# Start of a two-layer decoder kernel on one core: products of zeros ahead of the first tokens, one Newton chain for four blocks, and the first projection by contraction chunks in a written order

## The chip, the cores and the metric

The kernel runs on one core of a Trainium2 chip. The core has a matrix engine (PE, with a clock that the chip grants at one of two levels, 1.2 and 2.4 GHz), a vector engine (DVE), a scalar engine (ACT), GpSimd (POOL), and SyncE (SP), which issues nearly all DMA transfers. Each engine works through its own instruction list in order; engines wait for one another on semaphores. The metric is the device time of one execution in microseconds. For the kernel before, three executions gave a median of 1206.81 us (1206.57 to 1207.68).

## The reference

One sequence of 1024 tokens with 1024 features goes through two layers in float32. What the change touches is the head of the first layer:

```
h = rms_norm(x, g_in)                      # per token: x * rsqrt(mean(x^2) + eps) * g
z = h @ w_in                               # 256 cq | 128 ckv | 32 kpe | SWA q | SWA k | SWA v | gate
q = rms_norm(cq, g_q_a) @ w_q_up           # latent attention: low-rank queries
kv = rms_norm(ckv, g_kv_a) @ w_kv_up       #                   and keys and values
ang = positions * inv_freq                 # rotary angles, cos and sin of them turn q_pe and kpe
```

After that come dense causal latent attention with eight heads, sliding-window attention with eight heads, a gate and an output projection, then a second layer of forgetting attention with sixteen heads, its gate and output projection, and a last norm. None of the arithmetic of these is changed.

## The kernel before, in words

**Arithmetic.** Every float32 product is made of three products in a reduced float32 format: each operand is split into a high part, rounded, and a low part, the rest, and high times high, low times high and high times low are summed in one accumulator (`mm3`, L113 to L116). `split` (L99) makes the two parts from an accumulator bank: ACT casts the high part (L105), DVE subtracts it for the low part (L106). `split_sb` (L109) does it from on-chip memory: ACT casts, POOL subtracts (L111).

**Memory.** A table `TAGS` gives each kind of buffer a number of copies: raw weights `wr` have four, their high and low parts `wh` and `wl` three each. Accumulators live in eight banks, two each of `pj`, `s`, `t` and `o`.

**The start** (L510 to L800). Tokens come in blocks of 128; blocks 0 to 3 are the first half, 4 to 7 the second. `square_sum` (L141) sums squares on DVE or ACT, `inv_rms` (L118) makes the reciprocal root by an integer guess and three Newton steps, a chain of twelve small DVE instructions. `row_norm` (L560) runs it for blocks 0 and 1 together, then for block 2, then for block 3, and scales each block by its factor. `norm_T` (L200) turns the normed blocks: for each of eight contraction chunks of 128 features, four transposes on PE (products with the identity `ident`, L206) fill one bank, which is split into `hh` and `hl`. The first projection (`z_a`, the 256 columns of cq) takes blocks one after the other: per block 24 products of 256 columns into one `pj` bank (`token_project`, L181), a copy by DVE (L649), and a square sum. The second (`z_b`, 288 columns: ckv, kpe, SWA v) does the same per block into an `s` bank (copies at L698, L699, L702). The norms of cq and ckv follow (L682, L712), their transposes (L687) and splits, then the rotary tables: `rotary` (L541) computes sine and cosine on DVE and ACT, DVE copies them into four buffers `r0` (L728 to L732), PE turns each with four transposes (L735), and DVE copies the result out (L736). Next the rotated key (L746, L752), the SWA key projection (`swa_k`, weights `wh` and `wl`), and the up-projections (L771 copies their results).

**What sets the order.** In the start a scheduler decides in which order each engine takes its instructions, from its own estimate of when operands are ready; work of the two projections, transposes and small DVE chains is interleaved by it. `issue_after` holds some work back behind other work. For the main part a written list of units sets PE's order, and the scheduler sets that of the other engines.

## Time and profile before

| | |
|---|---|
| median of three executions | 1206.81 us (1206.57 to 1207.68) |
| the profiled execution | 1204.9 us, its span 1203.1 us |
| mean granted clock of PE, share of full speed | 0.993 |
| PE busy | 1161.3 us, 97% of the span, 6554 products and transposes |
| DVE, ACT, POOL busy | 738.1, 703.0 and 587.8 us (61, 58 and 49%) |
| data moved | 135.27 MB |

The span is the part of an execution that the trace covers; the rest of its time, 1.8 us, lies around it. An engine's busy share is a mean over very different stages. How to read the rows further below: a timeline row gives the start, the duration, the engine, the source line, the operation with what it writes and reads, the tile sizes, and how many such instructions follow one another; in brackets stands the idle time before it and what released it. Two rows of one engine can overlap, since instructions are pipelined: the pace is the distance between starts.

### The profile page before, as it was taken

To read this page: it belongs to the slowest core of one execution; us is meant where nothing else is said; L and a number is where in the kernel's file an instruction comes from. 1 tells how busy PE (TensorE), PEld (TensorE's weight loads), DVE (VectorE), ACT (ScalarE), POOL (GpSimd) and SP (SyncE) were. 2 spreads that over 40 slices of the span, in tenths; PEclk is the share of its full clock that TensorE was granted. 3 is DMA by queue.
4 is the path that set the end of the run, shared out by engine and by line. 5 is a ranking of instruction groups with operands and counts; after the bars stand their busy time and mean duration, and the time that the engine had idled before them with its cause. 6 is when DMAs were issued, how large, how long until landed. Compare 5 with 4: busy or idle time off the path is not lost. (4 is left out here: it accounts for less than half of the span.)

```text
span 1203.1 us, 19942 instructions
## 1 busy us (share of the span) xinstructions
PE 1161.3 (97%) x6554; PEld 1001.6 (83%) x6554; DVE 738.1 (61%) x1946; ACT 703.0 (58%) x1583; POOL 587.8 (49%) x737
## 2 busy tenths in 40 slices
PE   4999999999989999999999999999999999999997
PEld 4997888888878877889998888888888888877886
DVE  8955466676775776665004666666656666657754
ACT  5634477776764765664214667666767676766532
POOL 5501154564654554434204555656555555567452
PEclk9999999999998999999999999999999999999999
DMA  6326522453653443574313222313131223247541
GB/s 213 85 51 221 164 45 62 130 152 123 167 162 94 123 142 98 171 217 119 99 49 103 63 79 62 89 53 88 55 96 61 82 69 101 66 128 223 172 162 61
DMA packets 157084, 135.27 MB, mean 112 GB/s; under 512 B 53259, under 2 KB 121638, under 8 KB 156982
## 3 DMA queue, kind: packets, MB, share of 16 engines
q1 hardware_dynamic: 156982, 134.02, 37.0%
q8 instruction: 51, 0.84, 0.3%
q14 instruction: 51, 0.42, 0.1%
HBM read 96.43 MB, written 37.55 MB: 111 GB/s over the span
## 5 line engine op out<-in xcount | busy, mean ns | idle before, releaser
L114 PE MATMUL pj<-hh,wh 128*128 128x512 f32 (+1 forms) x792 | 321.8, 406 | 1.6 <-ACT wh L110 1.6
L116 PE MATMUL pj<-hh,wl 128*128 128x512 f32 (+1 forms) x792 | 310.9, 393 | 6.0 <-POOL wl L111 6.0
L115 PE MATMUL pj<-hl,wh 128*128 128x512 f32 (+1 forms) x792 | 310.3, 392 | 0.0
L111 POOL TENSOR_TENSOR wl<-wr,wh 128x512 fp32r<-128x512 f32 (+1 forms) x130 | 162.7, 1253 | 164.3 <-ACT wh L110 153.0
L103 DVE TENSOR_TENSOR pl<-t,ph 128x512 fp32r<-128x512 f32 (+1 forms) x320 | 179.0, 564 | 83.8 <-ACT ph L102 81.6
L276 POOL TENSOR_SCALAR r<-r,sm 128x128 f32<-128x128 f32 (+4 forms) x248 | 167.1, 681 | 127.5 <-DVE sm L323 77.5
L102 ACT CAST ph<-t 128x512 fp32r<-128x512 f32 (+1 forms) x320 | 153.6, 483 | 111.9 <-PE t L347 93.1
L116 PEld LDWEIGHTS pj<-hh,wl 128*128 128x128 f32 x792 | 149.6, 189 | 39.6 <-POOL wl L111 7.3
L321 ACT ACTIVATE r<-r,sm 128x128 f32<-128x128 f32 (+7 forms) x184 | 143.1, 778 | 54.2 <-DVE sm L314 52.3
L114 PEld LDWEIGHTS pj<-hh,wh 128*128 128x128 f32 x792 | 150.1, 190 | 23.7 <-ACT wh L110 2.4
L115 PEld LDWEIGHTS pj<-hl,wh 128*128 128x128 f32 x792 | 150.5, 190 | 20.5
L347 PE MATMUL t<-ident,r 128*128 128x128 f32 x828 | 136.1, 274 | 5.7 <-DVE pl L103 3.6
L347 PEld LDWEIGHTS t<-ident,r 128*128 128x128 f32 x828 | 103.9, 141 | 33.8 <-DVE pl L103 5.0
L110 ACT CAST wh<-wr 128x512 fp32r<-128x512 f32 (+1 forms) x130 | 77.8, 598 | 59.9 <-PE pj L115 30.8
L308 POOL TENSOR_TENSOR ld<-ld,zrow 128x128 f32<-128x128 f32 x128 | 58.7, 468 | 99.9 <-DVE sm L314 77.8
L338 PE MATMUL o<-ph,v 128*128 128x512 f32 (+3 forms) x288 | 107.2, 372 | 0.0
L339 PE MATMUL o<-pl,v 128*128 128x512 f32 (+3 forms) x288 | 99.7, 347 | 0.0
L314 DVE CUSTOM_DVE_ANT_0 r<-s,ld 128x512 f32<-128x512 f32 (+1 forms) x120 | 67.6, 563 | 47.2 <-PE s L261 43.4
L285 POOL TENSOR_TENSOR v<-ge,v 128x512 fp32r<-128x512 f32 x26 | 34.5, 1328 | 72.4 <-ACT v L284 71.2
L338 PEld LDWEIGHTS o<-ph,v 128*128 128x128 f32 x288 | 54.6, 190 | 7.8
L339 PEld LDWEIGHTS o<-pl,v 128*128 128x128 f32 x288 | 54.8, 190 | 6.3
L114 PE MATMUL pj<-qh,hh 128*128 128x256 f32 (+1 forms) x176 | 51.0, 291 | 2.9 <-DVE r L649 2.1
(324 smaller groups left out, 2450.3 us busy)
## 6 DMA issues: line engine op xcount, KB each, us to landing
wr<-in_o_w_in SPq DMA_DIRECT2D x62, 256.0 KB, 3.3
ld<-lcs SPq DMA_DIRECT2D x16, 512.0 KB, 4.0
ogs<-og SPq DMA_DIRECT2D x28, 256.0 KB, 2.1
wr<-ogs SPq DMA_DIRECT2D x28, 256.0 KB, 3.9
ge<-vscr SPq DMA_DIRECT2D x24, 256.0 KB, 3.7
gt<-x1s SPq DMA_DIRECT2D x23, 256.0 KB, 2.9
wr<-ogs SPq DMA_DIRECT2D x24, 192.0 KB, 3.1
wr<-in_e_w_in SPq DMA_DIRECT2D x16, 256.0 KB, 3.1
```

The costliest lines, as they stand in the source:

```text
L102: nc.scalar.copy(out=hi, in_=src)
L103: nc.vector.tensor_tensor(out=lo, in0=src, in1=hi.bitcast(F32), op=ALU.subtract)
L110: nc.scalar.copy(out=hi, in_=raw)
L111: (engine or nc.gpsimd).tensor_tensor(out=lo, in0=raw, in1=hi.bitcast(F32), op=ALU.subtract)
L114: nc.tensor.matmul(out=o, lhsT=ah, rhs=bh, start=first, stop=False)
L115: nc.tensor.matmul(out=o, lhsT=ah, rhs=bl, start=False, stop=False)
L116: nc.tensor.matmul(out=o, lhsT=al, rhs=bh, start=False, stop=last)
L276: nc.gpsimd.tensor_scalar(out=row, in0=row, scalar1=rc, scalar2=scale, op0=ALU.mult, op1=ALU.mult)
L321: nc.scalar.activation(out=row[:, 0:L], in_=row[:, 0:L], func=AF.Exp, scale=-1.0, bias=mn, accum_out=den)
L338: nc.tensor.matmul(out=O[0][:, cols], lhsT=v()[:, j, :], rhs=ph[:, cols], start=j == 0, stop=False)
L339: nc.tensor.matmul(out=O[0][:, cols], lhsT=v()[:, j, :], rhs=pl[:, cols], start=False, stop=j == n - 1)
L347: nc.tensor.transpose(out=t[:, b * P:(b + 1) * P], in_=rows[b][:, j * P:(j + 1) * P], identity=ident)
```

## The change

Ahead of everything else on PE stand 40 products of a zero tile (128 by 128, times 128 by 512, bf16). The first four blocks get one Newton chain, four wide; the square sum of the last block is halved between DVE and ACT, and the scaling is done in halves of 512 columns on POOL (block 0), ACT (block 1) and DVE (blocks 2 and 3). The first projection runs by contraction chunks: the four transposes of a chunk, then twelve products of an earlier chunk into four accumulators, two in `pj` and two in `o`. The order of PE, DVE, ACT and POOL up to there, and that of PE and DVE from there through the end of `swa_k`, is written out. In that second piece the rotary angles, the transposes of positions, the second half of the norms, `z_b`, the second half of `z_a`, the norms of cq and ckv and the rotary tables stand in one list. Raw weight buffers go from four to five for the whole kernel. The multiplications are the same apart from the 40.

```diff
+WARM = 40
...
-            "wr": (4, 2048), "wh": (3, 2048), "wl": (3, 2048),
+            "wr": (5, 2048), "wh": (3, 2048), "wl": (3, 2048),
...
+    def token_weight_steps(parts, pieces, cuts, tags_h, tags_l):
...
+                parts += [(wh[:, k + i, :], wl[:, k + i, :]) for i in range(m)]
+                yield
...
+    zeros = sbt("ob", [1024], BF16)
+    nc.vector.memset(zeros[:, 0:512], 0.0)
+    idle = pst("o")
+    with tc.manual_schedule(engines={mybir.EngineType.PE}):
+        for j in range(WARM):
+            nc.tensor.matmul(out=idle, lhsT=zeros[:, 0:P], rhs=zeros[:, 0:512], start=True, stop=True)
...
-    normed = row_norm(xrows, "VVAA", [(0, 2), (2, 1), (3, 1)], "VAVV")
-    za, _ = token_weights([(w0, 0, 256)], [(0, 4), (4, 4)], ["qh", "qh"], ["ql", "ql"])
+    za_raw = []
+    for k in range(0, KC, 2):
+        raw = sbt("wr", [2, 256])
+        load_cols(raw, [(w0, 0, 256)], k, 2)
+        za_raw.append(raw)
...
-            with tc.issue_after(normed):
-                normed = row_norm(rows, "AAAV", [(0, 1), (1, 3)], "PVVA")
...
+    def first_norm(hf):
...
+        yield from norm_T([lambda k, r=r: r[:, k * P:(k + 1) * P] for r in rows], hT[hf], 0)
...
+    def latent_q(hf):
+
+        accs = [pst("pj" if b < 2 else "o", 256) for b in range(4)]
+        hh, hl = hT[hf]
+        for k in range(KC):
+            wh, wl = za[k]
+            for m, (h, w) in enumerate(((hh, wh), (hl, wh), (hh, wl))):
+                for b in range(4):
+                    nc.tensor.matmul(out=accs[b], lhsT=h[:, k, b * P:(b + 1) * P], rhs=w, start=k + m == 0,
+                                     stop=(k, m) == (KC - 1, 2))
+            if k < KC - 1:
+                yield
...
+    def latent_kv(blk):
...
+    def norm_cq(hf):
+        y = inv_rms(ssq_q[hf], 4, 256)
+        for b in range(4):
+            nc.vector.tensor_scalar(out=cqs[hf][:, b, :], in0=cqs[hf][:, b, :], scalar1=y[:, b:b + 1],
+                                    scalar2=None, op0=ALU.mult)
...
+    def rotary_turn(hf, m):
+        cols, b4 = slice(hf * 512, (hf + 1) * 512), slice(4 * hf, 4 * hf + 4)
+        one, rot = (0, 64) if m == 0 else (64, 0)
+        cs = cs_raw[2 * hf + m]
+        nc.vector.tensor_copy(out=cs[:, :, rot:rot + 16], in_=cost[:, b4, :])
+        nc.vector.tensor_copy(out=cs[:, :, rot + 16:rot + 32], in_=cost[:, b4, :])
+        nc.vector.tensor_scalar(out=cs[:, :, rot + 32:rot + 48], in0=sint[:, b4, :], scalar1=-1.0,
+                                scalar2=None, op0=ALU.mult)
+        nc.vector.tensor_copy(out=cs[:, :, rot + 48:rot + 64], in_=sint[:, b4, :])
+        t = pst("s")
+        for b in range(4):
+            nc.tensor.transpose(out=t[:, b * P:(b + 1) * P], in_=cs[:, b, :], identity=ident)
+        nc.vector.tensor_copy(out=csEO[m][:, cols], in_=t)
+
+    ET = mybir.EngineType
+    with tc.manual_schedule(engines={ET.PE, ET.DVE, ET.Activation, ET.Pool}):
+
+        ssq = sbt("sm", [4])
+        part = sbt("sm", [2])
+        square_sum(xrows[0], ssq[:, 0:1], True)
+        square_sum(xrows[1], ssq[:, 1:2])
+        square_sum(xrows[2], ssq[:, 2:3])
+        square_sum(xrows[3][:, 0:512], part[:, 0:1], True)
+        square_sum(xrows[3][:, 512:D], part[:, 1:2])
+        nc.vector.tensor_scalar(out=ssq[:, 3:4], in0=part[:, 0:1], scalar1=part[:, 1:2], scalar2=None, op0=ALU.add)
+        y = inv_rms(ssq, 4, D)
+        for c in (slice(0, 512), slice(512, D)):
+            normalise(xrows[0][:, c], y[:, 0:1], 1.0)
+            nc.scalar.activation(out=xrows[1][:, c], in_=xrows[1][:, c], func=AF.Copy, scale=y[:, 1:2])
+            for b in (2, 3):
+                nc.vector.tensor_scalar(out=xrows[b][:, c], in0=xrows[b][:, c], scalar1=y[:, b:b + 1],
+                                        scalar2=None, op0=ALU.mult)
+            if c.start == 0:
+                g_ps = pst("pj", 32)
+                nc.tensor.transpose(out=g_ps[:, 0:19], in_=gst[0:19], identity=ident[0:19, 0:19])
+                nc.vector.tensor_copy(out=gains, in_=g_ps[:, 0:19])
+        for k in range(0, KC, 4):
+            wh, wl = sbt("qh", [4, 256], F32R), sbt("ql", [4, 256], F32R)
+            za += [(wh[:, i, :], wl[:, i, :]) for i in range(4)]
+            for i in (0, 2):
+                split_sb(wh[:, i:i + 2, :], wl[:, i:i + 2, :], za_raw[(k + i) // 2])
+
+        turns, steps = first_norm(0), None
...
+            made = next(turns, None) or made
+            if k == 1:
+                steps = latent_q(0)
+            if k > 1:
+                next(steps)
...
+            if k > 5:
+                for _ in range(2):
+                    next(zb_steps, None)
...
+    with tc.manual_schedule(engines={ET.PE, ET.DVE}):
+        p_ps = pst("pj", 32)
+        nc.tensor.transpose(out=p_ps[:, 0:NB], in_=posf, identity=ident[0:NB, 0:NB])
+        nc.vector.tensor_copy(out=post, in_=p_ps[:, 0:NB])
+        nc.vector.tensor_scalar(out=nsinks, in0=sinks, scalar1=-1.0, scalar2=None, op0=ALU.mult)
+        angles = chain(rotary(sint, 0.0), rotary(cost, 0.25))
+        turns = first_norm(1)
+        norm_cq(0)
+        for b in range(4):
+            for _ in range(2):
+                next(turns, None)
+            latent_kv(b)
+            next(angles)
+        norm_ckv(0)
+        for _ in latent_q(1):
+            pass
+        csEO = [sbt("r1", [S])]
+        latent_kv(4)
+        turn_cq(0)
+        csEO.append(sbt("r1", [S]))
+        norm_cq(1)
+        rotary_turn(0, 0)
+        latent_kv(5)
+        turn_ckv(0)
+        rotary_turn(0, 1)
+        latent_kv(6)
+        turn_cq(1)
+        rotary_turn(1, 0)
+        latent_kv(7)
+        norm_ckv(1)
+        rotary_turn(1, 1)
+        for hf, _ in enumerate(swa_k()):
+            if hf == 7:
+                turn_ckv(1)
...
-    cT = [(sbt("qh", [S], F32R), sbt("ql", [S], F32R)) for _ in range(2)]
...
-            acc = pst("s", 288)
...
-            with tc.issue_after(made):
-                nc.vector.tensor_copy(out=cs[:, :, rot:rot + 16], in_=cost[:, b4, :])
...
```

The change adds some lines, so that in the rows of order the same code has a higher line number after than before (the helper lines by 2 to 8).

PE's list at the start, after (first) and before (second). `pj`, `o`, `s` and `t` are accumulator banks, `qh` and `ql` the first projection's weights, `hh` and `hl` the turned tokens, `r` the blocks; the change has, behind the 40 products, the transpose of the gains and eight transposes of two chunks:

```order
L214 MATMUL s48_282<-ident_128,r12_69 128x128
L214 MATMUL s48_282<-ident_128,r13_71 128x128
L214 MATMUL s48_282<-ident_128,r14_73 128x128
L214 MATMUL s48_282<-ident_128,r15_75 128x128
L642 MATMUL pj49_289<-qh37_249,hh42_262 128x256
L642 MATMUL pj50_290<-qh37_249,hh42_262 128x256
L642 MATMUL o51_291<-qh37_249,hh42_262 128x256
L642 MATMUL o52_292<-qh37_249,hh42_262 128x256
L642 MATMUL pj49_289<-qh37_249,hl43_263 128x256
```

Before, after the first sixteen transposes (block by block, four chunks each):

```order
L114 MATMUL pj96_469<-qh33_173,hh46_235 128x256
L115 MATMUL pj96_469<-ql34_174,hh46_235 128x256
L114 MATMUL pj98_497<-qh33_173,hh46_235 128x256
L115 MATMUL pj98_497<-ql34_174,hh46_235 128x256
L206 MATMUL s52_265<-ident_82,r12_69 128x128
L206 MATMUL s52_265<-ident_82,r13_71 128x128
```

Four blocks now advance together, where two did. The next place is the first of the four rotary turns in the second piece. On PE, after, between the end of block 4 of `z_b` (into `pj134`) and the start of block 5 (into `pj149`), with `r174` the normed cq and `r085` the first rotary table:

```order
L118 MATMUL pj134_894<-kx80_496,hl95_545 128x288
L683 MATMUL t139_928<-ident_128,r174_482 128x128 x4
L683 MATMUL t142_937<-ident_128,r174_482 128x128 x4
L723 MATMUL s148_969<-ident_128,r085_510 128x128 x4
L116 MATMUL pj149_975<-kh63_405,hh94_544 128x288
```

On DVE, after, the end of the list between block 4 of `z_b` and the copy of the turned table. Ahead of these rows stand block 4's two copies, the two low parts of the turned cq (`ql138`, `ql141`) and the first eleven instructions of the Newton chain (`sm`) for the second half of cq (`r1126`):

```order
L139 TENSOR_TENSOR sm147_948<-sm147_948,sm145_946 128x4
L140 SCALAR_TENSOR_TENSOR sm146_947<-sm147_948,sm146_947 128x4
L674 TENSOR_SCALAR r1126_878<-r1126_878,sm146_947 128x256 x4
L716 COPY r085_510<-og10_153 128x4x16
L717 COPY r085_510<-og10_153 128x4x16
L718 TENSOR_SCALAR r085_510<-og11_154 128x4x16
L720 COPY r085_510<-og11_154 128x4x16
L724 COPY r1132_892<-s148_969 128x512
```

Before, DVE had the last copies of the cosines (`og9`) into the four tables far ahead of the end of `z_b`:

```order
L556 TENSOR_SCALAR gt15_116<-gt15_116 128x128
L728 COPY r0187_1178<-og9_110 128x4x16
L729 COPY r0187_1178<-og9_110 128x4x16
L728 COPY r0189_1190<-og9_110 128x4x16
L729 COPY r0189_1190<-og9_110 128x4x16
L728 COPY r0191_1202<-og9_110 128x4x16
L649 COPY r1104_581<-pj106_583 128x256
```

The table's copies now stand behind the Newton chain and the scaling of the second half of cq, and PE's list has the table's transposes ahead of the next block. The third place is POOL's list in the middle of the first layer, where weights of the gate (`wl`) and of a later key projection (`kx`) are split. Before:

```order
L276 TENSOR_SCALAR r1999_4393<-r1999_4393,sm1004_4406 128x640
L111 TENSOR_TENSOR kx1039_4510<-wr1041_4512,kx1037_4508 128x512
L111 TENSOR_TENSOR kx1039_4510<-wr1042_4517,kx1037_4508 128x512
L285 TENSOR_TENSOR v1063_4588<-ge1062_4586,v1063_4588 128x8x64
L276 TENSOR_SCALAR r11011_4429<-r11011_4429,sm1021_4457 128x768
L276 TENSOR_SCALAR r11024_4467<-r11024_4467,sm1029_4480 128x896
L111 TENSOR_TENSOR kx1040_4511<-wr1043_4522,kx1038_4509 128x512
L111 TENSOR_TENSOR kx1040_4511<-wr1044_4527,kx1038_4509 128x512
L111 TENSOR_TENSOR wl1053_4552<-wr1051_4549,wh1052_4551 128x512
```

After:

```order
L113 TENSOR_TENSOR wl1045_4573<-wr1043_4570,wh1044_4572 128x512
L113 TENSOR_TENSOR wl1048_4579<-wr1046_4576,wh1047_4578 128x512
L284 TENSOR_SCALAR r1991_4414<-r1991_4414,sm996_4427 128x640
L113 TENSOR_TENSOR kx1031_4531<-wr1033_4533,kx1029_4529 128x512
L113 TENSOR_TENSOR kx1031_4531<-wr1034_4538,kx1029_4529 128x512
```

The two `wl` splits moved ahead of the `kx` splits.

## Rows read from the trace of the kernel before

**Rows 1.** Page, engines: busy us, share of the span, instructions.

```profile
PE 1161.3 (97%) x6554; PEld 1001.6 (83%) x6554; DVE 738.1 (61%) x1946; ACT 703.0 (58%) x1583; POOL 587.8 (49%) x737
```

**Rows 2.** Windows: length, busy PE, PEld, DVE, ACT, POOL; granted clock, DMA share, GB/s.

```profile
0.00:12.40 12.40, 0.53 (x2) 0.36 (x3) 7.75 (x30) 5.94 (x9) 8.96 (x37) 1.00 0.83 291
...
363.00:369.00 6.00, 6.00 (x21) 4.91 (x21) 0.00 (x0) 0.62 (x1) 3.89 (x4) 0.60 0.84 187
...
130.00:1203.00 1073.00, 1050.11 (x5865) 902.01 (x5863) 651.71 (x1692) 641.89 (x1426) 545.37 (x645) 0.99 0.36 108
```

**Rows 3.** Timeline of PE in the start.

```profile
19.75 0.58 PE L114 MATMUL pj<-qh,hh 128*128 128x256 f32 x1
...
23.79 0.28 PE L115 MATMUL pj<-ql,hh 128*128 128x256 f32 x1
23.91 0.28 PE L114 MATMUL pj<-qh,hh 128*128 128x256 f32 x1
...
30.96 0.39 PE L114 MATMUL pj<-qh,hh 128*128 128x256 f32 x1 [1.29 <-DVE r L649]
...
57.42 1.04 PE L687 MATMUL t<-ident,r 128*128 128x128 f32 x8
```

**Rows 4.** Timeline of ACT in the start.

```profile
8.79 1.06 ACT L146 ACTIVATE ge<-r 128x1024 bf16<-128x1024 f32 x1 [0.18 <-DMA r<-in_x]
...
10.54 1.15 ACT L569 ACTIVATE r<-r,sm 128x1024 f32<-128x1024 f32 x1
11.60 1.64 ACT L110 CAST qh<-wr 128x512 fp32r<-128x512 f32 x3
...
19.01 0.69 ACT L105 ACTIVATE hh<-s,gains 128x512 fp32r<-128x512 f32 x1 [4.17 <-PE s L206]
```

**Rows 5.** Timeline of DVE, 56 to 76 us: norms of cq, latent splits, a Newton chain.

```profile
56.42 1.14 DVE L682 TENSOR_SCALAR r<-r,sm 128x256 f32<-128x256 f32 x4
...
68.21 1.41 DVE L106 SCALAR_TENSOR_TENSOR ql<-t,gains,qh 128x512 fp32r<-128x512 f32 x2 [3.45 <-ACT qh L105]
...
72.46 0.29 DVE L698 COPY r<-s 128x128 f32<-128x128 f32 x1 [2.55 <-PE s L116]
...
72.77 0.16 DVE L123 TENSOR_SCALAR sm<-sm 128x4 f32<-128x4 f32 x1
...
74.95 0.88 DVE L712 TENSOR_SCALAR r<-r,sm 128x128 f32<-128x128 f32 x4
```

**Rows 6.** Timeline of POOL, weight splits of the second projection.

```profile
32.30 2.20 POOL L111 TENSOR_TENSOR kx<-wr,kx 128x288 fp32r<-128x288 f32 x2 [1.75 <-ACT kx L110]
```

**Rows 7.** Timeline of DVE, 32 to 51 us: rotary instructions and table copies.

```profile
32.87 0.84 DVE L542 TENSOR_SCALAR ph<-gt 128x128 f32<-128x128 f32 x1
...
37.45 0.22 DVE L542 TENSOR_SCALAR ph<-gt 128x128 f32<-128x128 f32 x1
...
50.16 0.20 DVE L728 COPY r<-og 128x64 f32<-128x64 f32 x1 [0.38 <-ACT og L558]
```

**Rows 8.** Timeline of ACT, square sum of a 128-column block.

```profile
61.86 0.31 ACT L146 ACTIVATE ge<-r 128x128 bf16<-128x128 f32 x1 [0.90 <-DVE sm L136]
```

**Rows 9.** Timeline of PE, waits in the second half of the start.

```profile
51.56 0.38 PE L114 MATMUL pj<-qh,hh 128*128 128x256 f32 x1 [0.84 <-DVE r L649]
...
96.90 0.51 PE L114 MATMUL pj<-qh,ph 128*128 128x512 f32 x1 [1.03 <-DVE r L771]
```

**Rows 10.** Timeline of PE, two long waits of the main part and what follows.

```profile
362.53 0.79 PE L116 MATMUL pj<-hh,wl 128*128 128x512 f32 x1 [4.98 <-POOL wl L111]
363.12 0.63 PE L114 MATMUL pj<-hh,wh 128*128 128x512 f32 x1
363.55 0.63 PE L115 MATMUL pj<-hl,wh 128*128 128x512 f32 x1
...
438.04 0.79 PE L347 MATMUL t<-ident,r 128*128 128x128 f32 x3 [1.85 <-DVE pl L103]
```

**Rows 11.** Timeline of POOL ahead of the first of these waits.

```profile
356.78 3.48 POOL L111 TENSOR_TENSOR kx<-wr,kx 128x512 fp32r<-128x512 f32 x2
```

More of the change, by code (lines that the diff above doesn't have):

```diff
@@ L2 @@
 from functools import partial
+from itertools import chain
 import numpy as np
@@ L558, in rotary @@
         nc.scalar.activation(out=dst, in_=r_r, func=AF.Sin)
[L560 to L577 removed]
+        yield
+    za_raw = []
[3 more added lines that the diff above has]
+        za_raw.append(raw)
     for blk in range(4, NB):
@@ L603, in trunk @@
     nsinks = cp.tile([P, 8], F32, name="nsinks")
-    g_ps = pst("pj", 32)
-    nc.tensor.transpose(out=g_ps[:, 0:19], in_=gst[0:19], identity=ident[0:19, 0:19])
     gains = cp.tile([P, 19], F32, name="gains")
-    nc.vector.tensor_copy(out=gains, in_=g_ps[:, 0:19])
     qts = dr.tile([8, P, S], F32, name="qts")
@@ L619, in trunk @@
     lcs = dr.tile([16, S], F32, name="lcs")
-    hT = []
-    for hf in range(2):
+    hT, made = [], None
+    def first_norm(hf):
         rows = xrows[4 * hf:4 * hf + 4]
-        if hf:
-            with tc.issue_after(normed):
-                normed = row_norm(rows, "AAAV", [(0, 1), (1, 3)], "PVVA")
         hT.append(new_hT())
-        made = norm_T([lambda k, r=r: r[:, k * P:(k + 1) * P] for r in rows], hT[hf], 0)
-    with tc.issue_after(normed):
-        rotary(sint, 0.0)
-        rotary(cost, 0.25)
@@ new lines, in trunk, with turn_cq @@
+    cT = []
+    def norm_cq(hf):
[3 more added lines that the diff above has]
+                                    scalar2=None, op0=ALU.mult)
+    def turn_cq(hf):
+        for c in range(2):
+            if hf == 0:
+                cT.append((sbt("qh", [S], F32R), sbt("ql", [S], F32R)))
+            t = pst("t")
+            for b in range(4):
+                nc.tensor.transpose(out=t[:, b * P:(b + 1) * P], in_=cqs[hf][:, b, c * P:(c + 1) * P],
+                                    identity=ident)
+            cols = slice(hf * 512, (hf + 1) * 512)
+            split(cT[c][0][:, cols], cT[c][1][:, cols], t, gains[:, 16 + c:17 + c])
@@ new lines, in norm_ckv, with turn_ckv @@
+    def norm_ckv(hf):
+        y = inv_rms(ssq_kv[hf], 4, 128)
+        for b in range(4):
+            nc.vector.tensor_scalar(out=ckv[0][:, 4 * hf + b, :], in0=ckv[0][:, 4 * hf + b, :],
+                                    scalar1=y[:, b:b + 1], scalar2=None, op0=ALU.mult)
+    def turn_ckv(hf):
+        if hf == 0:
+            cT.append((sbt("v", [S], F32R), sbt("v", [S], F32R)))
+        t = pst("t")
+        for b in range(4):
+            blk = hf * 4 + b
+            nc.tensor.transpose(out=t[:, b * P:(b + 1) * P], in_=ckv[0][:, blk, :], identity=ident)
+        cols = slice(hf * 512, (hf + 1) * 512)
+        split(cT[2][0][:, cols], cT[2][1][:, cols], t, gains[:, 18:19])
@@ new lines, in trunk, with swa_k @@
+    swa = {}
+    def swa_k():
+        swa["k"] = sbt("kh", [S], F32R), sbt("kl", [S], F32R)
+        swa["kx"] = new_kx()
+        yield from project([(w0, KS, KS + P)], hT, stack_k(*swa["k"], swa["kx"]))
+    def rotary_turn(hf, m):
[8 more added lines that the diff above has]
+        t = pst("s")
+        for b in range(4):
+            nc.tensor.transpose(out=t[:, b * P:(b + 1) * P], in_=cs[:, b, :], identity=ident)
+        nc.vector.tensor_copy(out=csEO[m][:, cols], in_=t)
@@ new lines, in trunk @@
+    kpe = sbt("gt", [NB, 32])
+    cs_raw = [sbt("r0", [4, P]) for _ in range(4)]
+    for i, cs in enumerate(cs_raw):
+        one = 0 if i % 2 == 0 else 64
+        nc.gpsimd.memset(cs[:, :, one:one + 64], 1.0)
+    with tc.manual_schedule(engines={ET.PE, ET.DVE}):
[6 more added lines that the diff above has]
+        norm_cq(0)
+        for b in range(4):
+            for _ in range(2):
[4 more added lines that the diff above has]
+        for _ in latent_q(1):
+            pass
+        csEO = [sbt("r1", [S])]
[16 more added lines that the diff above has]
+                turn_ckv(1)
@@ L706, in trunk @@
-    cT.append((sbt("v", [S], F32R), sbt("v", [S], F32R)))
-    for hf in range(2):
-        y = inv_rms(ssq_kv[hf], 4, 128)
-        t = pst("t")
-        for b in range(4):
-            blk = hf * 4 + b
-            nc.vector.tensor_scalar(out=ckv[:, blk, :], in0=ckv[:, blk, :], scalar1=y[:, b:b + 1],
-                                    scalar2=None, op0=ALU.mult)
-            nc.tensor.transpose(out=t[:, b * P:(b + 1) * P], in_=ckv[:, blk, :], identity=ident)
-        cols = slice(hf * 512, (hf + 1) * 512)
-        split(cT[2][0][:, cols], cT[2][1][:, cols], t, gains[:, 18:19])
@@ L790, in up_v @@
         nc.sync.dma_start(out=vscr0[tok], in_=st)
-    swa = {}
     chunks = [{"gt": [None, None]} for _ in range(4)]
-    for _ in swa_k():
-        pass
     for pr in range(4):
@@ L1015, in next_norm @@
         hT_next.append(new_hT())
-        norm_T(parts, hT_next[hf], 8)
+        for _ in norm_T(parts, hT_next[hf], 8):
+            pass
     def out0(nh, blk):
```

124 lines of the change are left out of this document (41 added, 83 removed).

## Prediction

> **What bounds the kernel now.** I read the engines' table first: PE is busy 97% of the span, the next engine 61% [rows 1], so time is gained or lost only where PE stands still or runs at the lower clock. The windows say where that is [rows 2]: in the first 12.4 us PE works 0.53 us; over the 1073 us after 130 us it is idle 22.9 us in all. Third, the timelines of PE, ACT and DVE in the start [rows 3 to 9] show what each wait is for: PE waits for the first tokens, then for copies and norms on DVE. Fourth, the one long wait in the middle, 4.98 us for POOL [rows 10, 11]. The change writes 40 products of zeros into the empty 12.4 us and reorders the start; the multiplications stay, so the sum is made of PE's waits and of its clock.
>
> **A. The first projection starts earlier.** The fourth block's square sum begins at 8.79 [rows 4]. Halved, it takes about 0.63 us, between 0.31 for 128 columns and 1.06 for 1024 [rows 4, 8], and about 0.3 for reading out and adding: 9.7. One four-wide Newton chain takes 2.18 (72.77 to 74.95 [rows 5]): 11.9. ACT scales block 1 in two halves, about 1.25 where one piece took 1.15: 13.1. Its list then has four weight casts (three took 1.64, so 2.2) and the first high part (0.69): 16.0 [rows 4]. Before, the first such product stood at 19.75 [rows 3]: 3.7 earlier. From there eight chunks of twelve products 0.12 apart (23.79 to 23.91) and five times four transposes at about 0.11 [rows 3] make 11.5 + 2.2, with 0.3 for the first low part: the first half of z_a ends at 30.0. Before, by the same list, PE had at 29.7 two of the four blocks done and four transposes more; 1.29 of waiting [rows 3], 48 products and less those four transposes put the same work at 36.3. The lead is 6.3 us. Bounds: 4 if ACT's squares or casts push the high parts back, 8 if nothing ahead of 16.0 costs what I put.
>
> This needs PE at the upper clock by 16 us. Before, the first product at 19.75 took 0.58, and at 23.79, four us of products and transposes later, they took 0.28 and stood 0.12 apart [rows 3]. At the half level products of 512 columns stand 0.43 apart [rows 10]. If the zeros raise the level as soon as that work did, ten of them pass at 0.43 and thirty at 0.24, and the 40 end near 12, before the turned chunks can begin (about 13.6, when the halves are scaled). If they never do, they take 17.2 and end near 18.4. No row before shows a product of zeros. The Trainium skill's page "TensorE: Matmul & The Clock Gate" (Part 1, "What's actually happening") says that the gate goes by how busy PE has been, so zeros count like data; by that rule A stands at 6.3, and the other case is the second rival. No run here shows it yet.
>
> **B. The second stage, 30 us on.** The written list runs the second half's transposes (32) and four blocks of z_b (96 products of 288 columns). PE's own work is 32 x 0.10 + 96 x 0.134 = 16.1 (the transposes from eight in 0.79 between starts, the products scaled from 0.12 by 288/256 [rows 3]). In the same stretch DVE's list has, up to the copy that frees block 3's bank: four copies of 256 columns (0.29 each, as the scaling), a Newton chain 2.18, four scalings 1.14, eight low parts at 0.70, four latent copies at 0.31 [rows 5], and three half chains of rotary instructions, about 1.3, 1.9 and 1.3 at 0.22 to 0.3 each [rows 7]. That is 15.8, as much as PE. But small DVE instructions stretch while POOL splits weights: the same line took 0.84 at 32.87, beside POOL's split at 32.30, and 0.22 at 37.45 [rows 6, 7]. POOL has eight such splits here, so I add 3 to 5 us. Besides, those splits (0.8 to 1.1 each [rows 6]), behind three scalings, finish near 36, and block 0 of z_b wants them from 31 on: about 1.9. I take 6.8 for the waits of this stage, less the 0.84 that stood there [rows 9]: +6.0. Bounds: 1.1, if only the splits are waited for, and 7.8, if all stalls fall on PE. I lean to the upper end because the stretched rows are the nearest.
>
> **C. Four rotary turns.** PE cannot begin a block of z_b before the table's four transposes that its list has ahead of it, and those wait for DVE. Behind the first, DVE has after the end of block 4: the copies (0.31), two low parts, which wait for ACT's copy and square (0.31 each [rows 8]) and two high parts (0.69 pipelined to 0.57 [rows 4]), so that they end 2.9 after the block; then Newton 2.18, scalings 1.14, four small copies 0.45 [rows 5, 7]: 6.6. PE has 0.87 of transposes in the meantime: 5.7 idle. The second has one low part and the copies: 2.75 less 0.44, 2.3. The third two low parts and the copies: 3.35 less 0.87, 2.5. The fourth a square sum (0.75), Newton 2.18, four scalings 0.88, copies: 4.6 with handoffs, with nothing on PE beside it. Queued behind each is a whole block or swa_k, and for these wait DVE's next copies, so nothing catches up. Together 15.1, less 1.03 that stood before the first up-projection [rows 9] and 0.3 of small ones: +13.8. Bounds: 10.7 if the handoffs cost nothing, 18 if POOL's splits stretch these small instructions too.
>
> **D. The clock after these waits.** After the 4.98 us wait the next ten products stood 0.43 apart instead of 0.24 (twice 0.12, for twice the columns), and the window 363 to 369 was granted 0.60 [rows 2, 3, 10]: about 2.2 lost. The 1.85 us wait at 438.04 [rows 10] was followed by a similar stretch; that of 1.29 at 30.96 was not [rows 2, 3]. I count three such stretches (the 5.7, the 4.6 and the longest of B): +6.6. Bounds: 0 and 11 (five). The same page of the Trainium skill (Part 1, "HAM oscillation — how this bites in real kernels") tells of a kernel whose waits brought the half level back every time; the 4.98 here agrees, the 1.29 does not. [...]
>
> **E. Later: POOL's list at 356 us.** Before, PE waited 4.98 for `wl`, behind two `kx` splits that took 3.48 on POOL [rows 10, 11]. Now the `wl` splits stand ahead. I take 3.48 of the wait and its 2.2 of clock: -5.7. Bounds: 0, if the raw weights arrive as late or the `kx` parts are waited for in turn, and -7.2, if the whole wait goes with its clock.
>
> SP's list has the same transfers, and z_a's loads stood ahead of blocks 4 to 7 before, too. The fifth raw buffer lets later loads start earlier; no wait of PE in these rows is for such a load, so I cost it at nothing beyond E. The halved squares and the moved gains transpose lie on engines that wait in that stretch anyway.
>
> **Sum.** -6.3 + 6.0 + 13.8 + 6.6 - 5.7 = +14.4. On the profiled execution's 1204.9 that is 1219.3; the median of the runs lies 1.9 higher (1206.81), so 1221.
>
> **The rivals.** First, faster: the fifth buffer and POOL's new order pay in the whole main part. For it: POOL's weight splits own the longest wait there, and its list did change. The place is PE's 22.9 us of idle after 130 us [rows 2] and some 4 of half clock behind the two long waits. Against: the longest of that idle is the 4.98 that E has already, and the 1.85 at 438.04 is for DVE [rows 10], which no buffer touches. If three quarters went, 20 us with the clock, against A to C at +13.5 with the waits too scattered for D, the median would be 1200. It decides once more than 13.5 comes back. Second, the change does not do what it says: zeros do not lift the clock. Then the zeros end at 18.4, the chunks start four later than I put, and run at half pace for the first 5 us (2.5 lost); A turns from -6.3 to about +1, and the median is 1228 to 1229. Third, no change: the ends of the bounds on one side, -6.3 + 1.1 + 10.7 + 0 - 7.2 = -1.7; it needs waits without clock loss, DVE undisturbed by POOL, and all of E.
>
> **How the numbers follow.** My forecast has 0.74, the first rival 0.10, the second 0.08, the third and what lies near it 0.08. The range runs from 1208, where D is nearly nothing and B low, to 1231, where D is at five stretches or the zeros fail. Within 0.2% (2.4 us) is about what a measurement of this kernel cannot tell from no change. Slower by more holds the forecast, the second rival and a part of the third: 0.85; faster 0.11; the same 0.04.
>
> **What would show it.** In the new trace: zeros 0.43 apart and then about half of that (A, second rival); the first product of z_a near 16 and the first half done near 30; four waits of PE for DVE ahead of the table's transposes, of about 5.7, 2.3, 2.5 and 4.6, all between 65 and 95 us (C); DVE's small rotary instructions several times their length beside POOL (B); granted clock under 1 in windows behind the long waits (D); the wait of 4.98 gone or short (E). I am wrong if the turns find their tables ready, which needs DVE to be ahead of PE there, or if PE's idle after 130 us falls by over 10.

## The result, and the profile after

| | before | after |
|---|---|---|
| median of four executions, us | 1206.69 (1205.75 to 1207.68) | 1221.18 (1219.65 to 1222.00) |
| ratio to before, 95% interval | | 1.0119 [1.0101, 1.0136] |
| profiled execution, its span, us | 1204.9, 1203.1 | 1220.4, 1218.6 |
| mean granted clock | 0.993 | 0.990 |

The change makes the kernel 14.5 us slower; 1221 was forecast. The page's engine line now reads as follows; it answers to [rows 1]. PE is busy 14 us more, with the same products and the 40 of zeros.

```profile
PE 1175.2 (96%) x6594; PEld 1007.4 (83%) x6594; DVE 727.3 (60%) x1921; ACT 701.9 (58%) x1585; POOL 593.6 (49%) x741
```

Windows of the start after the change; the columns are those of [rows 2].

```profile
12.40:30.50 18.10, 16.12 (x131) 15.22 (x129) 12.12 (x29) 13.07 (x25) 13.84 (x13) 1.00 0.42 140
30.50:54.00 23.50, 19.52 (x132) 18.24 (x130) 20.15 (x57) 13.29 (x46) 13.84 (x22) 0.93 0.39 107
54.00:66.00 12.00, 11.75 (x85) 11.75 (x86) 6.36 (x22) 3.37 (x20) 5.89 (x17) 0.86 0.52 115
66.00:77.00 11.00, 5.71 (x44) 5.28 (x42) 5.78 (x24) 3.44 (x13) 0.00 (x0) 0.92 0.02 6
77.00:83.00 6.00, 5.22 (x26) 5.22 (x27) 1.96 (x11) 0.00 (x0) 0.00 (x0) 0.59 0.00 0
83.00:102.00 19.00, 9.48 (x72) 8.77 (x70) 9.79 (x49) 3.42 (x12) 0.00 (x0) 1.00 0.08 20
102.00:107.00 5.00, 4.72 (x16) 3.97 (x17) 0.82 (x3) 0.62 (x1) 1.28 (x1) 0.66 0.34 73
```

Two things are to be seen: PE stands still for 5.3 us in the fourth window and 9.5 in the sixth, with POOL at rest; and the granted clock is far under 1 in the windows right behind, the fifth and the seventh.

The waits of PE up to 130 us after the change (what waited for what, sum, times, longest), and the one of the main part that answers to the 4.98 us of [rows 10]:

```profile
PE s L723 <- DVE r L720: 15.7, 4, 5.9
PE pj L642 <- ACT ob L666: 2.6, 2, 1.6
PE s L214 <- POOL r L284: 1.5, 1, 1.5
...
PE pj L116 <- ACT kx L112: 0.8, 1, 0.8
PE pj L117 <- POOL kx L113: 0.5, 1, 0.5
...
PE pj L118 <- POOL wl L113: 0.6, 1, 0.6
```

PE's timeline after the change: the zeros, the first transposes, the first products and the last of the first half of z_a, the two waits at the second half's accumulators, and the four turns.

```profile
1.18 11.60 PE L538 MATMUL o<-ob 128*128 128x512 bf16 x40 [1.18 <-DVE ob L534]
...
14.40 0.66 PE L214 MATMUL s<-ident,r 128*128 128x128 f32 x4 [1.45 <-POOL r L284]
...
16.40 0.50 PE L642 MATMUL pj<-qh,hh 128*128 128x256 f32 x2 [0.48 <-ACT hh L107]
...
30.25 0.40 PE L642 MATMUL o<-ql,hh 128*128 128x256 f32 x2
...
52.31 0.39 PE L642 MATMUL pj<-qh,hh 128*128 128x256 f32 x1 [1.09 <-ACT ob L666]
...
54.25 0.38 PE L642 MATMUL pj<-qh,hh 128*128 128x256 f32 x1 [1.55 <-ACT ob L666]
...
77.78 1.11 PE L723 MATMUL s<-ident,r 128*128 128x128 f32 x4 [5.91 <-DVE r L720]
...
86.32 0.66 PE L723 MATMUL s<-ident,r 128*128 128x128 f32 x4 [2.38 <-DVE r L720]
...
93.63 0.66 PE L723 MATMUL s<-ident,r 128*128 128x128 f32 x4 [2.60 <-DVE r L720]
...
102.28 0.95 PE L723 MATMUL s<-ident,r 128*128 128x128 f32 x4 [4.82 <-DVE r L720]
```

The first product is at 16.4 where it was at 19.75 [rows 3], and the first half of z_a ends at 30.5 by the pace of its products (the last starts at 30.37). By the place of a product in PE's list (transposes counted, zeros left out), the changed kernel is 21.3 us behind at the 625th (113.9 before, 135.1 after). Further on, the 1901st and the 2001st products stand so, before:

```profile
343.14 0.39 PE L116 MATMUL pj<-kx,wl 128*128 128x512 f32 x1
...
370.55 0.40 PE L115 MATMUL pj<-hl,wh 128*128 128x512 f32 x1
```

and after:

```profile
365.69 0.39 PE L118 MATMUL pj<-kx,wl 128*128 128x512 f32 x1
...
385.25 0.40 PE L117 MATMUL pj<-hl,wh 128*128 128x512 f32 x1
```

The lag falls from 22.6 to 14.7 between them: the wait of 4.98 [rows 10] and its half clock are gone. Of the 22.6, however, 0.8 is a wait for DVE that is new, a little ahead of the 1901st product:

```profile
364.73 0.66 PE L355 MATMUL t<-ident,r 128*128 128x128 f32 x4 [0.80 <-DVE pl L105]
```

At the 1890th product the lag was 21.5 (341.0 before, 362.5 after), so that the new order is worth 6.8 us there. At the end the lag is 15.5.

### The profile page after: what moved, and what is told of

Its sections match the earlier page's. It is cut to its first block, busy times and chain, and to the rows that moved or that the text cites. A ratio compares the mean times of both kernels' runs of the same rounds, so it can differ in the third digit from the quotient of the medians.

```text
span 1218.6 us, 20020 instructions
## 1 busy us (share of the span) xinstructions
PE 1175.2 (96%) x6594; PEld 1007.4 (83%) x6594; DVE 727.3 (60%) x1921; ACT 701.9 (58%) x1585; POOL 593.6 (49%) x741
## 5 line engine op out<-in xcount | busy, mean ns | idle before, releaser
L284 POOL TENSOR_SCALAR r<-r,sm 128x256 f32<-128x256 f32 (+4 forms) x250 | 170.5, 690 | 113.7 <-DVE sm L331 64.9
L112 ACT CAST wh<-wr 128x512 fp32r<-128x512 f32 (+1 forms) x130 | 77.8, 598 | 51.4 <-PE pj L117 22.6
L148 ACT ACTIVATE ge<-r 128x512 bf16<-128x512 f32 (+3 forms) x44 | 23.8, 541 | 68.0 <-DVE gt L663 29.3
```

Source lines behind the costliest of these rows:

```text
L112: nc.scalar.copy(out=hi, in_=raw)
L284: nc.gpsimd.tensor_scalar(out=row, in0=row, scalar1=rc, scalar2=scale, op0=ALU.mult, op1=ALU.mult)
```

## The experiments

The twelve were timed in three groups of four (e1 to e4, e5 to e8, e9 to e12), each on one chip beside the kernel before. A ratio is to the kernel before of the same group, with its 95% interval; between groups, and against the first result, the ratios are the fairer comparison.

| run | median us | before | ratio |
|---|---|---|---|
| e1_turns | 1204.46 | 1205.17 | 0.9992 [0.9980, 1.0005] |
| e2_fill | 1219.91 | 1205.17 | 1.0120 [1.0100, 1.0140] |
| e3_after_wr4 | 1228.99 | 1205.17 | 1.0190 [1.0169, 1.0212] |
| e4_before_wr5 | 1207.23 | 1205.17 | 1.0011 [0.9996, 1.0025] |
| e5_after_again | 1224.50 | 1205.70 | 1.0159 [1.0140, 1.0177] |
| e6_fill_again | 1218.99 | 1205.70 | 1.0115 [1.0094, 1.0136] |
| e7_no_zeros | 1225.29 | 1205.70 | 1.0160 [1.0139, 1.0181] |
| e8_best | 1198.88 | 1205.70 | 0.9949 [0.9936, 0.9962] |
| e9_best_no_zeros | 1199.71 | 1206.02 | 0.9951 [0.9934, 0.9969] |
| e10_best_wr4 | 1204.20 | 1206.02 | 0.9988 [0.9977, 0.9999] |
| e11_before_one_chain | 1210.95 | 1206.02 | 1.0043 [1.0029, 1.0058] |
| e12_turns_held | 1199.57 | 1206.02 | 0.9946 [0.9933, 0.9960] |

### e1_turns: the four turns moved

```diff
-        norm_ckv(0)
-        for _ in latent_q(1):
-            pass
-        csEO = [sbt("r1", [S])]
+        csEO = [sbt("r1", [S])]
+        for hf in range(2):
+            for m in range(2):
+                rotary_copy(hf, m)
+        norm_ckv(0)
+        for k, _ in enumerate(latent_q(1)):
+            if k in (4, 6):
+                rotary_turn(k // 2 - 2, 0)
...
         norm_cq(1)
-        rotary_turn(0, 0)
         latent_kv(5)
         turn_ckv(0)
         rotary_turn(0, 1)
         latent_kv(6)
         turn_cq(1)
-        rotary_turn(1, 0)
+        rotary_turn(1, 1)
         latent_kv(7)
         norm_ckv(1)
-        rotary_turn(1, 1)
```

`rotary_copy` is the part of `rotary_turn` with the four DVE instructions that fill a table.

> The changed kernel, with the four rotary turns moved: all copies into the tables stand on DVE ahead of norm_ckv(0), two turns stand inside latent_q(1), the other two behind latent_kv(5) and latent_kv(6), and norm_cq(1) behind latent_kv(4), norm_ckv(1) behind latent_kv(7), with no PE work waiting right behind them. Theory (terms C and D): PE's four waits of 15.7 us in all at the turns go, and two half-level stretches after them (about 2.1 and 1.7) with them: 1221.2 - 19.5 = about 1202. Rival (DVE is what bounds this stretch, the waits only move to the next reader of DVE): half or more comes back elsewhere, 1211 or more.

Measured: 1204.46, a ratio of 0.9992 where the changed kernel had 1.0119 in the first result: 1.3%, or some 15 us, less. No wait of PE at the turns is left in its trace. But the wait ahead of `latent_q(1)` grew to 4.3 us. PE's row of it, then DVE's row that it stood behind, then POOL's beside that one, in e1_turns:

```profile
57.20 0.46 PE L642 MATMUL pj<-qh,hh 128*128 128x256 f32 x1 [4.34 <-ACT ob L666]
```

```profile
50.79 3.21 DVE L555 TENSOR_SCALAR ph<-gt 128x128 f32<-128x128 f32 x1
54.03 0.23 DVE L557 TENSOR_SCALAR ph<-ph 128x128 f32<-128x128 f32 x1
```

```profile
51.12 2.79 POOL L113 TENSOR_TENSOR ld<-wr,ld 128x256 fp32r<-128x256 f32 x4
```

The instruction at 50.79 took 3.21 us where its like took 0.23. It started at the end of a memset on POOL, 0.33 us ahead of four weight splits (2.79 us), and ended with these; block 3's copies, and behind them ACT's, which frees the bank, stood behind it. In the changed kernel the same instruction took 0.34 at 49.75, since there the four splits began 0.35 us after its end. Terms C and D hold, and the small part of the rival is this wait.

### e2_fill and e6_fill_again: products of zeros in front of the turns

```diff
+        pulse(20)
         rotary_turn(0, 0)
...
+        pulse(6)
         rotary_turn(0, 1)
...
+        pulse(7)
         rotary_turn(1, 0)
...
+        pulse(16)
         rotary_turn(1, 1)
```

`pulse(n)` issues n products of zeros like those at the start; the zero tile gets a buffer of its own.

> The changed kernel, with further products of zeros on PE in front of the four turns: 20, 6, 7 and 16, which fill 4.3, 1.3, 1.5 and 3.5 us of the 5.9, 2.4, 2.6 and 4.8 us that PE waits there. They do no work. Theory (term D: the half level follows from the idle time): the half-level stretches at 75 and 102 us go, the waits' ends stay, 1221.2 - 3.8 = about 1217.5. Rival (the level does not hang on what PE does in the wait, or zeros do not hold it): 1221.

> The kernel of e2_fill again (further products of zeros in front of the four turns), beside the changed kernel this time, since its one trace showed no half level anywhere and 5.8 us less, but its median stood as far above before as that of the changed kernel. Theory (term D): 3 to 4 us under the changed kernel of this call. Rival (other executions fall to the half level elsewhere, so zeros buy nothing on the whole): within 1.5 us of it.

> The changed kernel itself, on the same chip as the next three, so that they can be compared with it: both theories expect 14 to 15 us above the kernel before, about 1220.

Measured: e2_fill's trace has a clock of 1.00 in all windows of the start, a span of 1212.8, and its median is no lower against before than that of the changed kernel, 1.0120 to 1.0119. In one group with the changed kernel it is: e6_fill_again 1218.99 to e5_after_again 1224.50, 5.5 us less. Here are two windows of e6_fill_again behind the first and the last turn, to be held against 0.59 and 0.66 above:

```profile
77.00:83.00 6.00, 5.50 (x38) 4.60 (x38) 2.12 (x13) 1.15 (x4) 0.00 (x0) 1.00 0.01 3
...
102.00:107.00 5.00, 5.00 (x26) 4.16 (x25) 0.00 (x0) 0.67 (x2) 1.22 (x1) 1.00 0.00 0
```

The changed kernel's second profile, of e5_after_again, has the same waits at the turns and a span of 1226.9 instead of 1218.6:

```profile
PE s L723 <- DVE r L720: 15.7, 4, 5.9
```

```profile
12.40:30.50 18.10, 14.97 (x105) 14.57 (x106) 14.54 (x32) 12.95 (x25) 10.51 (x10) 0.81 0.47 155
30.50:54.00 23.50, 21.00 (x154) 19.21 (x153) 17.30 (x51) 12.10 (x42) 14.17 (x22) 1.00 0.38 104
54.00:66.00 12.00, 9.35 (x53) 9.09 (x53) 9.16 (x29) 4.82 (x26) 8.04 (x21) 0.72 0.49 102
...
80.00:88.00 8.00, 6.15 (x29) 6.16 (x30) 2.95 (x15) 0.00 (x0) 0.00 (x0) 0.57 0.00 0
88.00:107.00 19.00, 11.99 (x69) 11.28 (x67) 7.53 (x35) 3.42 (x12) 0.00 (x0) 0.82 0.04 11
107.00:115.00 8.00, 5.21 (x16) 4.30 (x17) 3.09 (x16) 0.62 (x1) 1.28 (x1) 0.57 0.31 67
```

The waits are a property of the kernel; how much of the half level follows on them differs from one execution to the next, by 7.0 of the 8.3 us between these two (half of PE's busy time at the half level in the start: 7.2 and 14.2 us). That is why e2_fill alone told nothing, with the changed kernel timed in another group. With both in one group the theory holds: zeros in the waits keep the clock, and they buy 5.5 us. The turns themselves wait as long: in the profiles the first comes at 77.50, as it does without them (77.78), and the second at 84.16 instead of 86.32, because the block between them runs at the full level. The half level behind the turns cost 3.8 us in the first profile of the changed kernel and 8.3 in the second, and nothing in e6_fill_again's. The 5.5 us hold for that group only: the changed kernel's own ratio went from 1.0119 in the first result to 1.0159 there, and e6_fill_again's 1.0115 is no lower than the first of these.

### e3_after_wr4, e4_before_wr5 and e10_best_wr4: the fifth raw buffer

```diff
-            "wr": (5, 2048), "wh": (3, 2048), "wl": (3, 2048),
+            "wr": (4, 2048), "wh": (3, 2048), "wl": (3, 2048),
```

This is the edit of e3_after_wr4 (on the changed kernel) and of e10_best_wr4 (on e8_best, below); e4_before_wr5 has the reverse on the kernel before.

> The changed kernel with four raw weight buffers, as before. Theory (term E is the fifth buffer, which lets the gate's weight splits stand ahead of the key splits on POOL): PE's wait of about 5 us for POOL near 370 us and its half-level stretch come back, 1221.2 + 8 = about 1229. Rival (the order of POOL there follows from the new start): about 1221.

> The kernel before with five raw weight buffers and nothing else. Theory (E is the fifth buffer alone): the wait of 4.98 us at 362.5 goes with its half-level stretch, 1206.7 - 8 = about 1199. Rival (E needs the new start): about 1206.7.

> The kernel of e8_best with four raw weight buffers. Theory (term E is the fifth buffer, whatever the start): the 5 us wait for POOL and its half level come back, +7 to +8, about 1206.5. Rival (with the start mended the scheduler finds the better order anyway): 1199.

Measured: without the fifth buffer the changed kernel takes 1228.99, near the 1229 expected. Against ratios of 1.0119 and 1.0159 with the buffer, 1.0190 is 8.6 or 3.7 us more, so the time alone is a loose measure. Its trace has the old wait back, and from the 1890th to the 2001st product it takes 6.8 us more than the changed kernel, as long as the kernel before. PE's row of the waits, in e3_after_wr4:

```profile
PE pj L118 <- POOL wl L113: 5.8, 3, 5.0
```

On e8_best it costs 4.7 us by the ratios, not quite the 7 to 8 (the profiles, 1198.4 and 1205.8, are 7.4 apart, 5.5 of it between the same two products). But the fifth buffer alone does not make the kernel before faster: 1207.23 to 1205.17. In e4_before_wr5 the wait at 362 goes too (7 us won between the 1901st and the 1976th product), and 5 us had been lost by 63 us. PE's, DVE's and POOL's rows there:

```profile
55.38 0.46 PE L114 MATMUL pj<-qh,hh 128*128 128x256 f32 x1 [3.21 <-DVE r L649]
```

```profile
44.73 3.80 DVE L554 TENSOR_SCALAR gt<-gt 128x128 f32<-128x128 f32 x1
```

```profile
45.57 2.82 POOL L111 TENSOR_TENSOR ld<-wr,ld 128x256 fp32r<-128x256 f32 x4
```

With a fifth buffer the second pair of these `ld` splits, at 52.49 in the kernel before, follows right on the first, and all four fall on one of DVE's rotary instructions. So E is the fifth buffer, as the theory had it, but the kernel before loses elsewhere what it wins there: 4.6 us by the 625th product and 7.5 by the 1901st, 1.3 of it in a wait just ahead of that one, as the changed kernel has it with 0.8; and some 4 us more behind the 4000th, to its profile's end.

### e7_no_zeros and e9_best_no_zeros: WARM = 0

```diff
-WARM = 40
+WARM = 0
```

> The changed kernel without the 40 products of zeros. Theory (term A: the zeros lift the clock before 14 us): PE begins its first transposes and products at the half level for some 4 to 5 us, the first half of z_a ends about 2.5 us later (33 instead of 30.5), and part of it is hidden by the waits for POOL and DVE behind it: 1 to 2.5 us slower than the changed kernel. Rival (the zeros gain nothing, since what follows at 30 us waits for POOL and DVE anyway): the same within 0.7 us.

> The kernel of e8_best without the 40 products of zeros. In e7_no_zeros their absence cost nothing that could be seen beside the long waits; here these are gone. Theory (PE waits for the first turned chunks anyway, and its transposes bring the clock up by 17.5 us): within 1 us of e8_best, about 1199.5. Rival (term A as predicted: the zeros save 2.5 us of half level): 1201.5.

Measured: 1225.29 to 1224.50 of the changed kernel, and 1199.71 to e8_best's 1198.88, of another group; the ratios to before are the same within a third of their intervals. The zeros at the start gain nothing that these runs can tell. PE's timeline of e7_no_zeros:

```profile
13.24 1.12 PE L214 MATMUL s<-ident,r 128*128 128x128 f32 x4 [3.42 <-POOL r L284]
...
16.18 0.79 PE L642 MATMUL pj<-qh,hh 128*128 128x256 f32 x2
...
17.59 0.40 PE L642 MATMUL o<-qh,hl 128*128 128x256 f32 x2
```

Without zeros POOL's scaling comes earlier (with them one of POOL's instructions waits for a transpose that stands behind the 40), the transposes begin at 13.24 at the half level, and the clock is up by 17.6. The first product stands at 16.18, no later than with the zeros, and the last of the first half of z_a starts at 30.59 instead of 30.37. The time of e7_no_zeros holds another loss besides, the one of e1_turns: the instruction that took 0.34 in the changed kernel takes 3.21, and PE waits 4.34 ahead of `latent_q(1)` where it had waited 1.09 and 1.55.

```profile
56.15 0.58 PE L642 MATMUL pj<-qh,hh 128*128 128x256 f32 x1 [4.34 <-ACT ob L666]
```

So e9_best_no_zeros beside e8_best is the cleaner pair. Nor do the zeros secure the clock: in e5_after_again they end at 12.0, PE stands still for 2.22 us ahead of its first transposes and for 1.16 ahead of the first product, and from 15.5 to 22.3 the clock is at the half level (0.81 in the window from 12.40 above). The last product of the first half of z_a starts at 33.20 there, later than without any zeros. The profiles of e3_after_wr4 and e10_best_wr4 have the same fall, from 14.2 and 15.1 on.

### e8_best and e12_turns_held: POOL's splits held back

```diff
-        nc.scalar.activation(out=dst, in_=r_r, func=AF.Sin)
+        sines.append(nc.scalar.activation(out=dst, in_=r_r, func=AF.Sin).ins)
...
-                    split_sb(hi[:, :, at:at + n], lo[:, :, at:at + n], src[:, :, a:a + n])
+                    with tc.issue_after(sines[1]):
+                        split_sb(hi[:, :, at:at + n], lo[:, :, at:at + n], src[:, :, a:a + n])
```

The same is done for the key and value weights. This, on top of e1_turns, is e12_turns_held. e8_best has besides:

```diff
-        accs = [pst("pj" if b < 2 else "o", 256) for b in range(4)]
+        accs = [pst("o" if b > 1 else "t" if hf else "pj", 256) for b in range(4)]
...
         latent_kv(4)
+        rotary_turn(0, 0)
         turn_cq(0)
...
         latent_kv(5)
+        rotary_turn(1, 0)
         turn_ckv(0)
-        rotary_turn(0, 1)
         latent_kv(6)
+        rotary_turn(0, 1)
         turn_cq(1)
-        rotary_turn(1, 1)
         latent_kv(7)
         norm_ckv(1)
+        rotary_turn(1, 1)
```

> The kernel of e1_turns with three edits more: the splits of the up-projections' weights are queued behind the second sine on ACT (and so behind DVE's rotary instructions on POOL, which took 3.21 us for one of them beside such splits), the second half of z_a accumulates in banks t and o instead of pj and o, so that it doesn't wait for the copies of block 3 of z_b (4.3 us in e1_turns), and all four turns stand behind blocks 4 to 7. Theory (what was left of B in e1_turns is this wait and its half-level stretch): 4.3 + 1.7 less than e1_turns, about 1198.5, faster than before by 6. Rival (POOL's splits are in the way wherever they stand): the wait moves behind 60 us, and the time stays near 1204.

> The kernel of e1_turns with one edit more: the splits of the up-projections' weights queued behind the second sine on ACT. Banks and turns are as in e1_turns. Theory (what cost e1_turns 4.3 us ahead of latent_q(1) was DVE standing 3.21 us in one instruction beside POOL's splits): the wait falls to about 1, with its half level, 1204.5 - 5 = 1199.5, near e8_best. Rival (the wait is for the bank, and other banks were what helped e8_best): 1204.

Measured: 1198.88 and 1199.57, both as expected. In e12_turns_held the instruction that had taken 3.21 takes 0.62, with POOL's splits behind 55 us, and the wait is 1.97 (about 1 was expected):

```profile
49.29 0.62 DVE L557 TENSOR_SCALAR ph<-gt 128x128 f32<-128x128 f32 x1
```

```profile
53.12 0.38 PE L644 MATMUL pj<-qh,hh 128*128 128x256 f32 x1 [1.97 <-ACT ob L668]
```

The one edit of e12 gives all of the 5 us (ratios 0.9946 and, in e1_turns, 0.9992); other banks and places of the turns add nothing that shows. In e8_best PE is not idle for a moment in the stretch of the turns, at the full clock:

```profile
66.00:100.00 34.00, 34.00 (x210) 30.56 (x210) 20.88 (x74) 17.94 (x43) 4.67 (x4) 1.00 0.35 86
```

e8_best is 0.5% faster than the kernel before (6.8 us), the best that was found; e9 and e12 are not to be told from it.

### e11_before_one_chain: one Newton chain on the kernel before

```diff
-    normed = row_norm(xrows, "VVAA", [(0, 2), (2, 1), (3, 1)], "VAVV")
+    normed = row_norm(xrows, "VVAA", [(0, 4)], "PAVV")
```

> The kernel before with one Newton chain for the first four blocks, and block 0 scaled by POOL; nothing else. Theory (the lead of term A comes from the norm of four blocks together, which ends the small DVE instructions of blocks 2 and 3 that stood 1.2 to 1.3 us each beside POOL's splits): the first product starts some 3 us earlier and 2 to 3 us of it last to the end, about 1203.5 where before is 1205.7. Rival (the lead comes from the chunks, which keep PE busy as soon as one chunk is turned): 1205.7.

Measured: 1210.95, 4.9 us slower than before; both theories fail. DVE and POOL in e11_before_one_chain:

```profile
11.24 1.24 DVE L137 TENSOR_TENSOR sm<-sm,sm 128x4 f32<-128x4 f32 x1
...
14.95 1.18 DVE L137 TENSOR_TENSOR sm<-sm,sm 128x4 f32<-128x4 f32 x1
```

```profile
11.19 4.93 POOL L111 TENSOR_TENSOR ql<-wr,qh 128x512 fp32r<-128x512 f32 x4 [0.84 <-ACT qh L110]
17.03 1.67 POOL L276 TENSOR_SCALAR r<-r,sm 128x1024 f32<-128x1024 f32 x1 [0.91 <-DVE sm L138]
```

Four links of the chain take 1.2 us each, as long as one of the four splits that POOL runs beside them. POOL's scaling of block 0 waits for the end of the chain, and PE's first transposes wait for that scaling; before, they had begun at 12.40:

```profile
18.75 1.11 PE L206 MATMUL s<-ident,r 128*128 128x128 f32 x4 [8.90 <-POOL r L276]
```

At the 129th product the kernel is 4.1 us behind the kernel before. The changed kernel's chain is the same, and its links take 0.16:

```profile
11.18 0.16 DVE L138 TENSOR_TENSOR sm<-sm 128x4 f32<-128x4 f32 x1
```

There POOL is at rest from 7.1 to 13.03, as it waits for a transpose that stands behind the 40 products, and the written order puts the first projection's splits behind the scaling (without the 40, in e7_no_zeros, POOL is at rest from 10.3 to 12.2 and the chain's links are as short, 0.16 to 0.27):

```profile
13.03 0.48 POOL L958 TENSOR_SCALAR bs<-d 128x256 f32<-128x256 f32 x1 [5.89 <-PE pj L746]
```

Beside POOL's splits one chain did not pay; what part of term A's lead is this order and what part the chunks, no run here separates.

## Why the prediction was right

**A.** Held in size: the first product at 16.4 against 16.0, the first half done at 30.5 against 30.0, a lead of 5.8 us against 6.3. Its condition did not hold: "This needs PE at the upper clock by 16 us" is wrong, since without zeros e7_no_zeros has the first product at 16.18 and the end of that half 0.2 us later. The zeros did lift the clock (40 in 11.60 us, where 17.2 was the figure for the half level); but three us of half-paced transposes lie where PE waits for ACT's first high part in any case. So in the second rival the 2.5 us for half pace were too much; the rest of its price, zeros that end at 18.4 and hold all else back, was not put to a test by runs that have no zeros. What part of the 5.8 comes from the chain and the written order, and what from the chunks, is open.

**B.** Too large by 2.5 us: of the 6.8 of waits, 4.3 came (2.6 for the banks of z_a, 0.8 and 0.5 for the last weights, 0.4 in two small ones). The weights cost 1.3 where I had 1.9, and DVE stood less: of the rotary instructions, one at 47.99 took 1.10 us, where it took 0.25 at 55.58. The upper bound of 7.8 does not follow from its parts (1.9 and 5, less 0.84, are 6.1). But the mechanism that I priced at 3 to 5 us is there, and where an edit moves POOL's splits onto the wrong DVE instruction, e1_turns and e7_no_zeros show what it takes: 4.3 us in one place. That the changed kernel escaped this by 0.35 us was luck.

**C.** Held: 5.91, 2.38, 2.60 and 4.82 were measured where 5.7, 2.3, 2.5 and 4.6 were forecast, in all 15.7 to 15.1. With the turns moved all of it went. This is the term that decided; it came out of PE's list and of DVE's, with durations of the trace before.

**D.** Held in size, in part by luck: the first profile has four stretches of half clock in the start (about 3.4 us of PE's work each, and 4.2 behind the first turn), 7.2 us lost to 6.6 forecast. Three of them stand where I put them, behind the 5.91, the 4.82 and the longest wait of B. The fourth, at 37.6, follows on waits of 0.8 and 0.5, while the longer 2.4 and 2.6 of the middle turns had none. In e5_after_again all four turns were followed by one, two more stand ahead of them, and 14.2 us were lost, over my bound of 11. It is a cost with a spread. The section "HAM oscillation — how this bites in real kernels" (Part 1) of the Trainium skill's page "TensorE: Matmul & The Clock Gate" tells of waits of about 3 to 5 us, each of them followed by the half level. The 5.91 and 4.82 here agree with it in both profiles; the 2.38 and 2.60, shorter than those it tells of (as is the 1.29 of the forecast), were followed by the half level in e5_after_again and not in the first profile, with granted clock 1.00 from 83 to 102.

**E.** Too small: the lag fell by 6.8 us, where 5.7 was forecast and 7.2 was the bound. The whole wait, all of its half clock (2.7 us) and a wait of 0.84 for ACT beside it went, and waits of 0.80 and 0.73 came in their place. I laid it to the order of POOL's list, which is right; e3 and e10 show that the fifth buffer sets this order. "I cost it at nothing beyond E" failed on the kernel before, where the same buffer loses elsewhere what it wins there (e4).

**The sum.** In spans, -5.8 for A, +3.5 for B (4.3 less 0.84), +14.4 for C (15.7 less 1.03 and 0.3), +7.2 for D give 19.3, and the 625th product is 21.3 late; for the 2 us between them I have no place (PE's gaps of under 0.2 us from 30.5 to 130 are 0.5 us in all). Less 6.8 for E, and with 1 us of small waits elsewhere, 15.5 remain, where 14.4 were forecast. B and E came out lower than forecast, by 2.5 and 1.1; A, C and D came out higher by 0.5 to 0.6 each, and the 3 us that no term held made up the rest. So the median, 1221.18 for 1221, is closer than the working deserves; in another group the same kernel was 18.8 us above the kernel before.

**The rivals.** The first, a gain from the fifth buffer in the whole main part, fails: PE's idle time behind 130 us fell from 22.9 to 19.9 us, the 4.98 of E less some new small waits. The second does not arise. The third, no change, needed B at 1.1, C at 10.7, D at nothing and all of E; of these only E came near.

## What to carry to other kernels

In an order that is written by hand, read each engine's list against the others': a PE instruction that waits for the end of a chain on DVE holds back all that is queued behind it, so put the chain's other work behind the instruction that PE waits for, or give PE independent work in between. Where a page shows a small DVE instruction several times its usual length, look at what POOL ran beside it, and move that, not the instruction. Compare kernels with long waits side by side only, since the half clock behind the waits comes and goes.

## What was not expected of the hardware

A small DVE instruction beside POOL's splits can take as long as several of them: 3.21 us beside the end of a memset and four splits of 2.79 in all (e1_turns), 3.80 beside the like and four of 2.82 (e4_before_wr5), against 0.23. In e11_before_one_chain four links of a chain took about one split each, 1.18 to 1.24; why a link stood for one split only, and those instructions for four, no run here shows. The Trainium skill's page "SBUF — State Buffer" (section "Who interferes with whom") says that DVE and GpSimd share a pair of ports, which whoever issues first holds for its whole instruction. The 1.2 us agree with that; the 3.21 and 3.80, over four instructions that follow one another, are longer than one instruction, and there the measurement decides.

The same kernel, with the same waits at the turns to a tenth of a microsecond, took 1218.6 and 1226.9 us in two profiled spans; 7.0 of the 8.3 us between them are work at the half level (mean granted clock 0.990 and 0.983). Products of zeros in the waits took the half level away at the turns.
